# Block products in all four quarters of both MLPs, with sums that grow in PSUM, in a two-layer encoder on one core

## The chip, the core and the metric

The kernel runs on one core of a Trainium2 chip. TensorE (PE) multiplies, VectorE (DVE), ScalarE (ACT) and GpSimd (POOL) work element by element, and SyncE (SP) issues most of the transfers. Matmuls write to PSUM, which has eight banks of 128 x 512 fp32 values; everything else lies in SBUF. The metric is the device time of one execution in microseconds.

## What is computed

An encoder of two layers over a sequence of 512 with width 1024, all in fp32. Each layer is a mixer and an MLP, both behind an RMS norm and with a residual. The mixer of layer 0 is a stick-breaking attention, that of layer 1 a gated linear recurrence. The change touches both MLPs, the beginning of the recurrence and the final norm. Of the reference:

```python
def rms_norm(x, g):
    y = xf * lax.rsqrt(jnp.mean(xf * xf, axis=-1, keepdims=True) + EPS)
    return (y * g.astype(jnp.float32)).astype(x.dtype)
...
def rglru_block(h, w_in, conv_w, conv_b, w_a, b_a, w_x, b_x, lam, w_o):
    proj = h @ w_in
    gate = jax.nn.gelu(proj[..., :RG_WIDTH])
    xc = causal_depthwise_conv(proj[..., RG_WIDTH:], conv_w, conv_b)
...
def squared_relu_mlp(h, w1, w2):
    u = jax.nn.relu(h @ w1)
    return (u * u) @ w2
...
    for layer in range(DEPTH):
        h = rms_norm(x, norm_mix[layer])
...
        x = x + y
        h = rms_norm(x, norm_mlp[layer])
        x = x + squared_relu_mlp(h, mlp_w1[layer], mlp_w2[layer])
    return rms_norm(x, norm_final)
```

w1 is 1024 x 4096 and w2 is 4096 x 1024.

## The kernel before

**Numbers in two parts.** A matmul in full fp32 is replaced by three of a faster form: each operand is split into a high part (an ACT cast, `wh`, `xgh`, `bh`) and the remainder (a DVE subtraction, `wl`, `xgl`, `bl`), and high x high, low x high and high x low are added in PSUM (`three`, lines 193 to 197). A weight slab of 1024 x 128 (`slab`, line 174) is one transfer of 512 KB, a cast and a subtraction; `dense` (line 199) multiplies it with eight chunks of the input, 24 matmuls of 512 columns into one bank. `beside` (line 207) does so for several slabs at once, chunk by chunk, and takes the norm's matmul (line 149: ones times the sum of squares, then a square root on ACT and a reciprocal on DVE, line 126) in the middle.

**Order.** PE's instructions run in the order in which the program writes them. The orders of the other engines' queues are set by a scheduler that simulates the program and takes, among what is ready, what was written first; `issue_after` and `high_priority` bend that.

**The MLP.** The class `Mlp` (line 686) works in four quarters of the 4096 hidden features. For a quarter, `squared` makes its eight chunks `u`: 24 matmuls, then relu times the norm on DVE (line 739) and a square on ACT. The first three quarters are multiplied with w2 by Winograd's form of a 2 x 2 block product: seven products of halves in place of eight. `sums` (line 747) makes the sums of blocks of `u`, `split` their two parts; `load` (line 774) fetches the blocks b11, b12 and b22 of the weights, and `down` (line 791) goes through the seven products. For each it adds a second block to the first where that is wanted (line 805), splits it (`operand`, line 782) and issues 24 matmuls (lines 812 to 814) into two banks of its own, and then collects the two banks into the product's piece in SBUF: copies on ACT in the first quarter (line 818), additions on DVE later (line 820). The banks go round over all eight (`BANKS`, line 697). After the third quarter `outputs` (line 822) makes the four blocks of the output from the seven pieces, with seven DVE operations.

**The fourth quarter** is plain. `plain` splits the eight chunks of `u`. In layer 0 they are multiplied with slabs (`residual(w_m2, "mix1")`, line 878): 24 matmuls for each output chunk, and behind each of them the residual add (line 662), the scaling and split for the next layer (`halves`, lines 117 and 118) and the square. The block outputs are transposed on PE in the quarter's `squared` stage (`between`, lines 864 to 875) and added to `x` there. In layer 1 (lines 1085 to 1133) the rows of the result are made in two column halves of four row blocks each, 24 matmuls of 512 columns apiece, the last one as two of 256 columns; behind the second half stand the final norm and the stores.

**The recurrence's beginning.** `dense_in` (line 947) multiplies slabs of w_in. The first two go side by side with the norm's matmul in their middle (line 953). `conv` multiplies its bank with the norm (line 962) and reads it in four taps (lines 970 and 972), splits the result and loads and splits the gates' weights; `gates` multiplies with them. The order is that of the list in lines 1035 to 1041. From the seventh slab on, the low part is made on POOL with an adding transfer (lines 187 and 188).

## Time and profile before

| | us |
|---|---|
| median of 3 runs (lowest to highest) | 1085.01 (1083.53 to 1085.39) |
| profiled execution | 1085.11 |
| its span, first to last instruction | 1083.4 |

The profiled execution's time is 1.7 us over its span. Granted TensorE clock over the span: 0.999. In the page's rows of time, 40 slices of 27.1 us each, DVE is busy 0.7 or more in most slices, ACT in the first ones and around the recurrence. A row of the timeline gives start, length, engine, line, operation, output and inputs with shapes; an x says how many instructions were merged, and brackets tell how long the engine was idle before and what released it. A group's row gives busy us and mean ns. Matmul records overlap, so the distance between two starts is the pace, not the length.

### The profile page before, as it was taken

Reading aid. Unit: us, or ns where it says so; the run is one execution under the profiler, and the core shown is the slowest. Engines: PE = TensorE matmul, PEld = TensorE weight load, DVE = VectorE, ACT = ScalarE, POOL = GpSimd, SP = SyncE. Lnnn points to the kernel's source line nnn. Section 1 sums busy time; section 2 is a strip of 40 time slices with the busy share of each in tenths; the row PEclk is TensorE's granted clock in tenths of the full one; section 3 lists DMA queues with packets and bytes.
Section 4 is the critical chain, followed back from the end, with each engine's and each line's share of the span. In section 5 each row is a group of like instructions: output and inputs, shape, how many; then the busy total and the mean of one; then the engine's idle time right before and its main releaser. Section 6 shows DMA issues by size and latency. Waiting matters only on the chain.

```text
span 1083.4 us, 13612 instructions
## 1 busy us (share of the span) xinstructions
PE 1070.0 (99%) x5052; PEld 888.6 (82%) x5052; DVE 772.1 (71%) x1001; ACT 562.0 (52%) x831; POOL 202.5 (19%) x213
## 2 busy tenths in 40 slices
PE   8999999999999999999999999999999999999997
PEld 6888888788888888888888788888888888888886
DVE  7788787839894597599466658975784696699632
ACT  6767676726455344344345467944455443443422
POOL 2344443420000000002223556021000000002220
PEclk9999999999999999999999999999999999999999
DMA  7744453426205305302334486242215215203402
GB/s 230 189 128 137 124 149 96 156 82 246 84 26 187 98 20 175 117 1 80 114 111 136 90 209 153 82 175 78 78 59 175 78 47 184 81 1 123 150 1 78
DMA packets 43170, 122.57 MB, mean 113 GB/s; under 512 B 7648, under 2 KB 8416, under 8 KB 43104
## 3 DMA queue, kind: packets, MB, share of 16 engines
q1 hardware_dynamic: 41088, 115.94, 34.1%
q0 software_dynamic: 1440, 5.24, 2.6%
q8 instruction: 40, 0.66, 0.2%
q10 hardware_dynamic: 576, 0.52, 0.1%
q14 instruction: 26, 0.21, 0.1%
HBM read 101.76 MB, written 2.10 MB: 96 GB/s over the span
## 4 chain that ended last, share of the span: by engine, by line
PE 92%; DMA 2%; DVE 2%; ACT 2%; issue 1%; SPq 0%; DVEq 0%; ACTq 0%
PE ps_acc L195 7%; PE ps_acc L196 7%; PE ps_acc L197 7%; PE ps_o L195 4%; PE ps_o L196 4%; PE ps_o L197 4%; PE ps_t L196 4%; PE ps_t L195 4%; PE ps_t L197 4%; PE ps_z L195 3%; PE ps_z L196 3%; PE ps_z L197 3%; PE ps_t L813 2%; PE ps_t L812 2%; PE ps_t L814 2%; PE ps_acc L813 2%
## 5 line engine op out<-in xcount | busy, mean ns | idle before, releaser
L184 ACT CAST wh<-raw 128x1024 fp32r<-128x1024 f32 (+2 forms) x144 | 128.1, 911 | 158.9 <-PE ps_acc L197 51.2
L190 DVE TENSOR_TENSOR wl<-raw,wh 128x1024 fp32r<-128x1024 f32 (+2 forms) x134 | 141.4, 1070 | 27.4 <-ACT wh L184 27.4
L745 POOL TENSOR_TENSOR bl<-u,bh 128x512 fp32r<-128x512 f32 x16 | 30.5, 1904 | 584.9 <-ACT bh L744 569.8
L195 PE MATMUL ps_acc<-xgh,wh 128*128 128x512 f32 x320 | 129.1, 403 | 0.5 <-ACT wh L165 0.5
L787 ACT CAST wh<-b 128x1024 fp32r<-128x1024 f32 x72 | 75.5, 1049 | 98.4 <-PE ps_acc L814 15.7
L196 PE MATMUL ps_acc<-xgh,wl 128*128 128x512 f32 x320 | 125.4, 392 | 1.1 <-DVE wl L166 1.1
L197 PE MATMUL ps_acc<-xgl,wh 128*128 128x512 f32 x320 | 125.3, 392 | 0.1
L788 DVE TENSOR_TENSOR wl<-b,wh 128x1024 fp32r<-128x1024 f32 x72 | 87.9, 1221 | 25.3 <-ACT wh L787 25.2
L512 DVE TENSOR_TENSOR_SCAN scan<-keep,later 128x128 f32<-128x128 f32 (+1 forms) x64 | 58.4, 914 | 21.3 <-ACT keep L504 13.5
L197 PEld LDWEIGHTS ps_acc<-xgl,wh 128*128 128x128 f32 x320 | 60.1, 188 | 13.5 <-DVE xgl L118 0.5
L196 PEld LDWEIGHTS ps_acc<-xgh,wl 128*128 128x128 f32 x320 | 60.3, 188 | 12.0 <-DVE wl L166 1.8
L195 PEld LDWEIGHTS ps_acc<-xgh,wh 128*128 128x128 f32 x320 | 60.1, 188 | 11.7 <-ACT wh L165 0.7
L740 ACT ACTIVATE u<-u 128x512 f32<-128x512 f32 x64 | 39.3, 629 | 53.3 <-DVE u L739 53.1
L195 PE MATMUL ps_t<-xgh,wh 128*128 128x512 f32 x168 | 66.1, 394 | 0.0
L196 PE MATMUL ps_t<-xgh,wl 128*128 128x512 f32 x168 | 65.7, 391 | 0.0
L197 PE MATMUL ps_t<-xgl,wh 128*128 128x512 f32 x168 | 65.5, 390 | 0.0
L516 POOL TENSOR_TENSOR w<-w,scan 128x128 f32<-128x128 f32 (+1 forms) x64 | 53.8, 842 | 50.8 <-DVE scan L512 48.1
L195 PE MATMUL ps_o<-xgh,wh 128*128 128x512 f32 x152 | 60.2, 396 | 0.0
L197 PE MATMUL ps_o<-xgl,wh 128*128 128x512 f32 x152 | 59.2, 390 | 0.0
L196 PE MATMUL ps_o<-xgh,wl 128*128 128x512 f32 x152 | 59.2, 390 | 0.0
L195 PE MATMUL ps_z<-xgh,wh 128*128 128x512 f32 x128 | 50.0, 391 | 0.0
L196 PE MATMUL ps_z<-xgh,wl 128*128 128x512 f32 x128 | 49.9, 389 | 0.0
(356 smaller groups left out, 2768.1 us busy)
## 6 DMA issues: line engine op xcount, KB each, us to landing
raw<-in_w_m SPq DMA_DIRECT2D x72, 512.0 KB, 3.5
b<-in_w_dn SPq DMA_DIRECT2D x36, 512.0 KB, 4.3
raw<-in_w_in SPq DMA_DIRECT2D x16, 512.0 KB, 4.0
raw<-in_w_qk SPq DMA_DIRECT2D x12, 512.0 KB, 3.6
raw<-in_w_dn SPq DMA_DIRECT2D x12, 512.0 KB, 3.5
wl<-raw POOLq DMA_DIRECT2D x10, 512.0 KB, 6.3
x<-in_xT SPq DMA_DIRECT2D x16, 256.0 KB, 4.7
raw<-in_w_ro SPq DMA_DIRECT2D x8, 512.0 KB, 3.9
```

Of the source, the lines that this page charges most:

```text
L184: A.copy(wh[:, k, :], raw[:, k, :])
L190: V.tensor_tensor(wl[:, k, :], raw[:, k, :], f(wh[:, k, :]), ALU.subtract)
L195: PE.matmul(ps, wh, ah, start=start, stop=False)
L196: PE.matmul(ps, wl, ah, start=False, stop=False)
L197: PE.matmul(ps, wh, al, start=False, stop=stop)
L512: V.tensor_tensor_scan(sc[:, S - n : S][:, ::-1], keep[:, :n][:, ::-1], later[:, S - n :][:, ::-1], 1.0, ALU.mult, ALU.max,)
L516: G.tensor_tensor(wt, wt, sc[:, S - n + 1 : S + 1], ALU.mult)
L740: A.activation(t, t, AF.Square)
L745: G.tensor_tensor(bl[:, c, :], t, f(bh[:, c, :]), ALU.subtract)
L787: A.copy(wh, raw)
L788: V.tensor_tensor(wl, raw, f(wh), ALU.subtract)
L813: PE.matmul(ps[i], h[:, piece, ts], wl[:, jj, :], start=False, stop=False)
```

## The change

All four quarters of both MLPs use the block products, so w2 is stored in blocks as a whole and `w_m2` and `w_last` go.

The seven products are collected into four outputs, not seven pieces. Products that an output needs together grow in PSUM: P1, P6, P7 and P4 in one pair of banks (X), P5 and P3 in a second (V), P2 alone in a third (W). After each product the pair's sum so far is collected into one output, added or subtracted; an output's first collect in a layer is an ACT copy, all others are on DVE. `outputs` goes.

In the last quarter P1, P5 and P2 run first for one half of the inner index and then for the other, and P4 is left to a function of the layer (`end`). A block sum whose product is named in `far` is made by an adding transfer from HBM on POOL's queue (P7 and P4 in layer 0, P4 in layer 1).

Layer 0's `end` transposes output chunks 4 to 7 between the two halves of P4, with residual add and split; then the first two slabs of w_in run side by side over chunks 4 to 7 and 0 to 3, and chunks 0 to 3 are transposed after their first and second steps. The squares follow in a burst. The norm's matmul moves to the middle of the third slab, conv 3 ahead of the first gates, and the banks of `dense_in` go in the order t, t, acc, acc in place of alternating. The gates' weights are loaded three ahead.

Layer 1's `end` finishes the first two row blocks ahead of P4, and gives P4's last half two banks of 256 columns of its own, so that the sum in X is collected before them.

```diff
-    def beside(srcs, ah, al, pss, sq, at):
+    def beside(srcs, ah, al, pss, at, ks=range(C)):
         ws = [slab(src) for src in srcs]
-        for k in range(C):
-            if k == at:
-                r = sq.inv_rms()
+        for i, k in enumerate(ks):
+            if i in at:
+                at[i]()
             for ps, (wh, wl) in zip(pss, ws):
...
+        PRODUCTS = {
+            "P1": (0, "b11", None, "X", 0, False),
+            "P5": (4, "b11", "b12", "V", 3, False),
+            "P6": (5, "b11", "b22", "X", 1, True),
+            "P3": (6, "b22", None, "V", 1, False),
+            "P7": (1, "b12", "b22", "X", 3, True),
+            "P2": (2, "b21", None, "W", 0, False),
+            "P4": (3, "b11", "b21", "X", 2, False),
+        }
...
+        def block(self, q4, name, g, far):
+            _, b, to, *_ = self.PRODUCTS[name]
...
+            raw = self.raws[b, g]
+            if name in far:
+                G.dma_start(out=raw, in_=self.weights(q4, g, to), accum_op=ALU.add)
+            elif to:
+                V.tensor_tensor(raw, raw, self.raws[to, g], ALU.add)
+            return self.operand(raw)
+
+        def times(self, name, g, i, w, ps, new, cols=slice(0, S)):
+            block = self.PRODUCTS[name][0]
+            ts = slice(i * P, (i + 1) * P)
+            wh, wl = w
+            for jj in range(2):
+                h, l = self.a[2 * g + jj]
+                first, last = new and g == jj == 0, g == jj == 1
+                for n, (x, y) in enumerate(((h, wh), (h, wl), (l, wh))):
+                    PE.matmul(
+                        ps, x[:, block, ts], y[:, jj, cols], start=first and n == 0,
+                        stop=last and n == 2, skip_group_check=not new,
+                    )
+
+        def collect(self, name, i, ps, cols=slice(0, S)):
+            out, less = self.PRODUCTS[name][4:]
+            y = self.c[out][:, i, cols]
+            if (out, i) in self.begun:
+                V.tensor_tensor(y, y, ps, ALU.subtract if less else ALU.add)
+            else:
+                self.begun.add((out, i))
+                A.activation(y, ps, AF.Copy, scale=-1.0 if less else 1.0)
+
+        def down(self, q4, far=(), end=None):
+            sums = {}
+            def product(name, g):
+                w = self.block(q4, name, g, far)
+                to = self.PRODUCTS[name][3]
+                new = name in ("P1", "P5", "P2")
+                if to not in sums:
+                    sums[to] = [self.bank() for _ in range(2)]
+                for i in range(2):
+                    self.times(name, g, i, w, sums[to][i], new)
+                if g:
+                    for i in range(2):
+                        self.collect(name, i, sums[to][i])
+            if end is None:
+                for name in ("P1", "P5", "P6", "P3", "P7", "P2", "P4"):
+                    for g in range(2):
+                        product(name, g)
+                return
+            for g in range(2):
+                for name in ("P1", "P5", "P2"):
+                    product(name, g)
+            for name in ("P6", "P3", "P7"):
                 for g in range(2):
+                    product(name, g)
+            end([self.block(q4, "P4", g, far) for g in range(2)], sums["X"])
...
     with ExitStack() as mctx:
         mlp = Mlp(mctx, 0, sq)
+        def feature(c, tag):
+            pt = bank(tag)
+            for t in range(NB):
+                PE.transpose(
+                    pt[:, t * P : (t + 1) * P], mlp.y(t, c // 4)[:, c % 4 * P : (c % 4 + 1) * P],
+                    ident,
+                )
+            add_x(c, pt)
+            last["low"] = halves("mix1", c, x[c])
+
+        def end(ws, xs):
+            for i in range(2):
+                for g in range(2):
+                    mlp.times("P4", g, i, ws[g], xs[i], False)
+                mlp.collect("P4", i, xs[i])
+                if i == 0:
+                    for c in range(4, C):
+                        feature(c, "zzaa"[c - 4].replace("a", "acc"))
+
+        mlp.quarters(lambda q4, c: None, ("P7", "P4"), end)
+
+        begin = [bank("t") for _ in range(2)]
+        beside(
+            [w_in[C], w_in[C + 1]], xgh, xgl, begin,
+            {
+                1: lambda: [feature(c, "z") for c in range(2)],
+                2: lambda: [feature(c, "o") for c in range(2, 4)],
+            },
+            (*range(4, C), *range(4)),
+        )
+        sq = Squares()
+        with tc.tile_pool(name="squares", bufs=C - 1) as pool:
+            for c in range(C):
+                sq.chunk(c, x[c], last["low"], pool)
...
             if r is None:
-                first.extend(bank(t) for t in ("acc", "t"))
-                r = beside([w_in[C], w_in[C + 1]], xgh, xgl, first, sq, 4)
+                first.append(bank("acc"))
+                beside([w_in[C + 2]], xgh, xgl, first[2:], {4: norm})
             turns[0] += 1
             if first:
                 return first.pop(0)
-            return dense(w_in[i], xgh, xgl, tag=("t", "acc")[turns[0] % 2])
+            return dense(w_in[i], xgh, xgl, tag=("t", "t", "acc", "acc")[(turns[0] - 1) % 4])
...
-            (conv, 0), (conv, 1), (conv, 2), (gate, 0), (gates, 0), (gates, 1), (conv, 3), (gates, 2),
-            (gate, 1), (conv, 4), (gates, 3), (recur, range(3)), (gate, 2), (conv, 5), (gates, 4),
+            (conv, 0), (conv, 1), (conv, 2), (gate, 0), (conv, 3), (gates, 0), (gates, 1), (gate, 1),
+            (gates, 2), (conv, 4), (gates, 3), (recur, range(3)), (gate, 2), (conv, 5), (gates, 4),
...
+        def end(ws, xs):
+            for t in range(2):
+                square(t, 0, 0)
+                scaled(t, 0)
+                square(t, 1, 1)
+                finish(t, 1, 1)
+            for t in range(2, 4):
+                square(t, 1, 0)
+                scaled(t, 1)
+            for g in range(2):
+                mlp.times("P4", g, 0, ws[g], xs[0], False)
+            mlp.collect("P4", 0, xs[0])
+            square(2, 0, 1)
+            finish(2, 0, 1)
+            mlp.collect("P4", 1, xs[1])
+            for i in range(2):
+                cols = slice(i * HS, (i + 1) * HS)
+                ps = mlp.bank()[:, :HS]
+                for g in range(2):
+                    mlp.times("P4", g, 1, ws[g], ps, True, cols)
+                mlp.collect("P4", 1, ps, cols)
+                square(3, 0, 1 + i, cols)
+                if i == 0:
+                    V.tensor_tensor(ss[:, 3, 0:1], ss[:, 3, 0:1], ss[:, 3, 1:2], ALU.add)
+                    scaled(3, 0, cols)
+            finish(3, 0, 2, HS)
+
+        mlp.quarters(between, ("P4",), end)
```

`square` is the square with its row sum on ACT, `scaled` the product with the final norm's gain on POOL, and `finish` the rest of the final norm of a row block with its two stores; they hold the operations of lines 1110 to 1133.

More of the change, by code (lines that the diff above doesn't have):

```diff
@@ L757, in split @@
             if j < 2:
-                n = PIECES * HS
+                n = BLOCKS * HS
                 h, l = (
@@ L846, in quarters @@
                 if last:
+                    self.down(q4, far, end)
                     break
-                ts = [self.squared(q4 + 1, c) for c in range(2)]
+                for c in range(2):
+                    self.squared(q4 + 1, c)
                 self.down(q4)
-                if q4 + 1 == NQ - 1:
-                    self.blocks.close()
-                    self.outputs()
-                    for c in range(2):
-                        self.plain(c, ts[c])
-                else:
-                    self.sums(0)
-                    self.split(0)
+                self.sums(0)
@@ L860, in hybrid_encoder @@
+                self.split(0)
+            self.blocks.close()
     with ExitStack() as mctx:
         mlp = Mlp(mctx, 0, sq)
[L862 to L875 removed]
@@ L877, in hybrid_encoder @@
-        mlp.quarters(between)
-        sq = residual(w_m2, "mix1")
+        last = {}
+        def feature(c, tag):
[15 more added lines that the diff above has]
+                        feature(c, "zzaa"[c - 4].replace("a", "acc"))
@@ L1061, in hybrid_encoder @@
     with ExitStack() as mctx:
+        lp = mctx.enter_context(tc.tile_pool(name="last", bufs=1))
         mlp = Mlp(mctx, 1, sq)
```

202 lines of the change are left out of this document (63 added, 139 removed).

## The prediction, made before the change was run

> **What bounds the kernel now.** I read the page first, then who TensorE (PE) waited for, then the order of time around the stages that the diff touches.
>
> ```profile
> span 1083.4 us, 13612 instructions
> PE 1070.0 (99%) x5052; PEld 888.6 (82%) x5052; DVE 772.1 (71%) x1001; ACT 562.0 (52%) x831; POOL 202.5 (19%) x213
> PEclk9999999999999999999999999999999999999999
> ```
>
> ```profile
> PE ps_t L534 <- DVE tl L550: 2.5, 3, 1.5
> ...
> PE ps_z L495 <- ACT keep L504: 0.5, 1, 0.5
> ```
>
> PE has work in 99% of the span at full clock, and the list of its waits (us in total, times, longest) is short: the largest is 2.5 us, and every row belongs to the attention block or the start. From the first MLP on PE never waits. So the time is PE's instruction stream laid end to end, plus the start and the tail, and two questions decide: how much of that stream goes, and whether the rest still runs without gaps. Busy time can't answer the first, since records of neighbouring matmuls overlap; the distance from start to start can.
>
> ```profile
> 391.63 0.39 PE L812 MATMUL ps_o<-wh,bh 128*128 128x512 f32 x1
> 430.56 0.40 PE L195 MATMUL ps_z<-xgh,wh 128*128 128x512 f32 x1
> ...
> 548.46 1.03 PE L871 MATMUL ps_o<-ident,c 128*128 128x128 f32 x8
> 549.25 0.48 PE L195 MATMUL ps_acc<-bh,wh 128*128 128x512 f32 x1
> 592.89 0.39 PE L195 MATMUL ps_acc<-xgh,wh 128*128 128x512 f32 x1
> ...
> 1033.08 0.48 PE L1103 MATMUL ps_acc<-wh,bh 128*128 128x512 f32 x1
> 1071.27 0.28 PE L1103 MATMUL ps_t<-wh,bh 128*128 128x256 f32 x1
> 1076.90 0.28 PE L1105 MATMUL ps_t<-wh,bl 128*128 128x256 f32 x1
> ```
>
> **What is removed from PE.** These are PE's rows at the borders of stages. A block-product quarter (from line 812) has 7 products of 24 matmuls, 168 in all: 430.56 - 391.63 = 38.93 us, 0.2317 us each, 5.56 us a product. The plain fourth quarter of layer 0 has 8 x 24 = 192: 592.89 - 549.25 = 43.64 us, 0.2273 us each. In layer 1 it is 168 of 512 columns, 1071.27 - 1033.08 = 38.19 us, and 48 of 256 columns, 5.63 us from the first to the last and one step of 0.12 more: 43.94 us together.
>
> After the change layer 0 runs 168 in 38.93 us: 4.71 us less. In layer 1 the last 12 are cut into 24 of 256 columns: 156 x 0.2317 + 24 x 0.12 = 39.03 us, 4.91 us less. **PE's stream loses 9.6 us.** The transposes (32 a layer) move and stay as many; the pair of slabs run side by side, the third slab and the norm matmul that follow layer 0 stay as many too.
>
> The Trainium skill's "TensorE: Matmul & The Clock Gate" (section "Wait — 56ns, not 53.3ns?") gives a warm matmul its columns at 2.4 GHz and about 2.5 ns, 215.7 ns for 512 columns, whatever the pattern. By it the 48 fewer matmuls would be worth 10.4 us; the rows show 227 and 232 ns, with the block form the dearer, so I keep 9.6.
>
> **The sums that grow in PSUM.** Before, each product had two banks of its own out of eight, and was collected (line 820, VectorE, DVE; line 818, ScalarE, ACT, in the first quarter) while three more products ran. Now P1, P6, P7, P4 share one pair of banks and P5, P3 another. Each of P6, P3, P7 and P4 must wait in PE's queue until the collect of the product before in that pair has read it, and all later matmuls stand behind it. One other product lies between, 5.56 us of cover.
>
> ```profile
> 396.93 0.39 PE L814 MATMUL ps_o<-wh,sl 128*128 128x512 f32 x1
> 397.62 0.68 DVE L820 TENSOR_TENSOR c<-c,ps_o 128x512 f32<-128x512 f32 x1
> 398.55 0.68 DVE L820 TENSOR_TENSOR c<-c,ps_o 128x512 f32<-128x512 f32 x1
> ...
> 507.48 0.40 PE L812 MATMUL ps_t<-wh,bh 128*128 128x512 f32 x1
> 507.55 0.67 DVE L820 TENSOR_TENSOR c<-c,ps_o 128x512 f32<-128x512 f32 x1
> 509.29 0.67 DVE L820 TENSOR_TENSOR c<-c,ps_o 128x512 f32<-128x512 f32 x1
> ```
>
> ```profile
> 391.00:430.00 39.00, 39.00 (x170) 31.63 (x169) 30.82 (x36) 17.38 (x17) 0.00 (x0) 1.00 0.40 132
> 474.00:513.00 39.00, 39.00 (x170) 31.62 (x169) 36.29 (x38) 17.04 (x18) 4.43 (x2) 1.00 0.14 46
> 955.00:998.00 43.00, 43.00 (x187) 34.92 (x186) 40.26 (x42) 18.66 (x20) 5.64 (x2) 1.00 0.15 50
> ```
>
> The product whose last matmul starts at 396.93 is collected by 399.23, 2.1 us after its slot ends at 397.16; the latest I found ends at 509.96, 2.5 us after the next product began at 507.48. Both leave over 3 us. In the windows (length, then busy PE, weight loads, DVE, ACT, POOL) DVE has 30.8 of 39 us in the second quarter, and 36.3 and 40.3 in the third, where it also works off the seven output sums of line 829, which go away. The quarter that becomes a block quarter then has the load of the second. In the first quarter, DVE takes over 6 of 14 collects from ACT, 4 us of 39. I cost the seven quarters with the product between at nothing; the cover is those 3 us, and if it went, every us of lateness would be paid up to four times a quarter.
>
> The Trainium skill's "PSUM — Partial Sum Buffer" speaks against this edit: in "PSUM bank collisions raise a hardware error" two engines must not touch one bank in the same partitions at once, so that reading and resuming can't overlap. By that the wait is real and can't be softened; the rows say that it ends in time.
>
> In the last quarter of each layer P4 follows P7 at once, in the same banks. Cover is the second half of P7's last six matmuls, 1.39 us. The collect starts about 0.4 us after its bank's last matmul and takes 0.68, so a free DVE is in time by 0.3 us, and one in the middle of a 1.22 us subtraction is late by up to 0.9. I take 0.25 us a layer, **0.5 us** (0 to 1.8).
>
> The blocks fetched by an adding DMA on POOL's queue replace DVE additions.
>
> ```profile
> L787 ACT CAST wh<-b 128x1024 fp32r<-128x1024 f32 x72 | 75.5, 1049 | 98.4 <-PE ps_acc L814 15.7
> ...
> L788 DVE TENSOR_TENSOR wl<-b,wh 128x1024 fp32r<-128x1024 f32 x72 | 87.9, 1221 | 25.3 <-ACT wh L787 25.2
> ...
> wl<-raw POOLq DMA_DIRECT2D x10, 512.0 KB, 6.3
> ```
>
> Such a transfer lands in 6.3 us (median of ten). P4's can go when P6's operands are split, before P6 runs; P6, P3 and P7 are 16.7 us, and 6.3 us with a cast and a subtraction (1.05 and 1.22) leaves 8. Nothing is queued behind it on POOL there. Cost nothing.
>
> **Layer 0 to layer 1.** Before, each output chunk came with 5.4 us of matmuls to itself, and its residual add, scaling, split and square hid there. Now all eight come together: 4 chunks transposed between the halves of P4, 4 between the first matmuls of the next layer's two slabs. The nearest rows are those of the first MLP's start, which handles its chunks in such a burst.
>
> ```profile
> 244.30:267.30 23.00, 23.00 (x103) 18.90 (x102) 21.99 (x31) 17.25 (x25) 0.00 (x0) 1.00 0.69 252
> ...
> 255.93 0.68 DVE L662 TENSOR_TENSOR x<-x,ps_acc 128x512 f32<-128x512 f32 x1
> 256.53 2.73 DVE L118 SCALAR_TENSOR_TENSOR xgl<-x,colt,xgh 128x512 fp32r<-128x512 f32 x4
> 266.50 0.68 DVE L145 TENSOR_TENSOR ssq<-ssq,sq 128x512 f32<-128x512 f32 x1
> 267.44 1.02 PE L149 MATMUL ps_z<-ssq,ones 128*128 128x512 f32 x2
> ...
> L190 DVE TENSOR_TENSOR wl<-raw,wh 128x1024 fp32r<-128x1024 f32 x86 | 105.8, 1232 | 24.9 <-ACT wh L184 24.9
> ...
> L145 DVE TENSOR_TENSOR ssq<-ssq,sq 128x512 f32<-128x512 f32 x7 | 4.8, 688 | 0.1
> ```
>
> There DVE was busy 22.0 of 23 us, and the last square was added at 267.18, in time for the norm matmul by its usual 0.26 us. From the end of P4's first half PE now has 16 transposes (0.1 us each, from the eight at 548.46), 12 matmuls, 48 of the pair at 5.60 us per 24, 16 transposes and 12 of the third slab before the norm: 1.6 + 2.8 + 11.2 + 1.6 + 2.7 = 19.9 us. DVE has two collects, 8 adds, 8 splits, 7 sums of squares and three slabs: 1.4 + 5.4 + 5.5 + 4.8 + 3.7 = 20.8, and starts 0.5 us late: **1.4 us** of waiting. It shows at the second slab's bank, which P4's second collect frees, or at the norm. It is 0 if the slabs' subtractions wait their turn (17.6 us), and 4 if the collect of P4's second half stands behind the first chunks' eight operations, which come earlier in the program.
>
> The norm's result is late next.
>
> ```profile
> 598.49 1.02 PE L149 MATMUL ps_z<-ssq,ones 128*128 128x512 f32 x2
> 600.27 3.35 DVE L126 RECIPROCAL r<-r 128x512 f32<-128x512 f32 x1 [4.21 <-ACT r L125]
> 604.44 0.70 DVE L962 TENSOR_TENSOR ps_acc<-ps_acc,r 128x512 f32<-128x512 f32 x1 [0.82 <-PE ps_acc L197]
> 606.34 0.78 ACT L970 ACTIVATE bt<-ps_acc,colt 128x512 f32<-128x512 f32 x1
> 609.80 0.74 DVE L972 SCALAR_TENSOR_TENSOR bt<-ps_acc,colt,bt 128x509 f32<-128x509 f32 x1
> 612.21 2.14 DVE L979 TENSOR_TENSOR bl<-bt,bh 128x512 fp32r<-128x512 f32 x2 [0.41 <-ACT bh L978]
> ```
>
> It comes 603.62 - 598.49 = 5.1 us after the norm matmul starts, and the first convolution then takes 6.1 us (604.44 to 610.54) until its bank is free, 11.2 us in all. Before, PE had other banks. Now conv 3 takes conv 0's bank, and PE reaches it after 0.9 us of norm (its row, 1.02, overlaps the next), 2.7 us of the third slab and 5.46 of gate 0: 9.0 us. **2.2 us** of waiting; 0 if conv 0 runs alone (0.70 + 0.78 + 3 x 0.75 = 3.7 us after the result), 4.3 if a third chunk is interleaved (three operations of 0.7 more). The gates follow 5.4 us later, at 16.7, behind the two low halves (done 15.9 after the norm): nothing more.
>
> **The end.**
>
> ```profile
> 1077.22 0.42 DVE L1108 TENSOR_TENSOR c<-c,ps_t 128x256 f32<-128x256 f32 x1 [1.53 <-PE ps_t L1105]
> ...
> 1079.97 0.38 SPq L1133 DMA_DIRECT2D out<-c  x1
> ```
>
> The chain after the last matmul keeps its operations. But the row block before it is finished with 2.9 us of matmuls left in place of 5.7, on the same ACT, DVE and SP queue: **0.5 us**, between 0 and 2.
>
> **The sum.** The profiled execution took 1085.11 us, 0.1 over the median of 1085.01. 1085.11 - 9.6 + 0.5 + 1.4 + 2.2 + 0.5 = **1080.1 us**; its own range, with half of each bound, is 1077.5 to 1083.
>
> **Rivals.** First, every new wait is covered: 1085.1 - 9.6 = 1075.5. For it, the first MLP's start, where the same burst cost PE nothing; against it, the bank that conv 3 takes 2 us too early by the rows.
>
> Second, the passage between the layers costs its upper bounds: 4 + 4.3 + 1.8 + 2 = 12.1 against 9.6, so 1087.6, and 1085 with some of them. For it, DVE's 96% in the window above; against it, a late PE gives DVE time, so the first two don't add in full.
>
> Third, on the slow side, one mechanism: the collects come late and PE stands at each resumed sum. There are 4 in each of 8 quarters, 32; a mean wait of 0.3 us eats the gain, from 0.37 it is slower by more than 2.2 us, and 0.5 gives 1085.1 - 9.6 + 16 = 1091.5. For it, DVE's 40.3 of 43 us in layer 1; against it, the collects above, 3 us early. That the matmuls weren't the pace, so that their removal gives nothing, PE's list of waits excludes.
>
> **Chances.** Forecast 0.53, all covered 0.21, the passage dear 0.17, late collects 0.09. The range 1075 to 1086 takes in the second and most of the third, and leaves out the fourth. About 0.2%, 2.2 us, is what this measurement can tell from no change; faster takes the first two but for the forecast's upper edge at 1083: 0.71; within 0.12, from that edge and the dear passage at 1085; slower 0.17, the rest of the dear passage and the late collects.
>
> **What would show it.** Right: in each fourth quarter 168 matmuls and some 39 us; no PE waits at the resumed sums but P4's; a PE wait for DVE at the norm or the second slab's bank, and one of about 2 us at the first matmul of conv 3. Wrong: waits at P6, P3 or P7 in every quarter; a fourth quarter with waits for operands or for the adding DMAs; a tail over 8 us.

## The result, and the profile after

The changed kernel is slower by 0.4%: a median of 1088.66 us (1088.48 to 1089.49, 5 runs) beside 1084.77 for the kernel before, ratio 1.0041 with a 95% interval of 1.0026 to 1.0055. The forecast was 1080.1 us, with a range that ended at 1086. Its profiled execution took 1088.52 us. Page and list of PE's waits (us in total, times, longest) of the changed kernel:

```profile
span 1086.3 us, 13618 instructions
...
PE 1062.0 (98%) x4992; PEld 880.9 (81%) x4992; DVE 824.7 (76%) x1081; ACT 569.3 (52%) x823; POOL 167.1 (15%) x196
```

```profile
PE ps_t L193 <- DVE bt L1024: 5.9, 1, 5.9
...
PE ps_z L147 <- DVE ssq L143: 2.3, 1, 2.3
PE ps_t L824 <- DVE sl L776: 1.9, 1, 1.9
PE ps_t L193 <- DVE c L833: 1.2, 1, 1.2
...
PE ps_t L824 <- DVE c L833: 0.3, 1, 0.3
```

PE is busy for 8 us less than before, so the products did go; but a list that held nothing behind the attention block now holds four waits of over 1 us there, 11.3 us together. The row of a few tenths at line 824 is all that the resumed sums cost. Where the waits lie, PE's timeline shows, with the norm matmuls (line 147; 149 before) as marks:

```profile
265.73 0.59 PE L147 MATMUL ps_z<-ssq,ones 128*128 128x512 f32 x1
...
543.99 0.39 PE L824 MATMUL ps_t<-wh,bh 128*128 128x512 f32 x1
...
580.97 1.03 PE L897 MATMUL ps_z<-ident,c 128*128 128x128 f32 x8
...
587.55 0.50 PE L193 MATMUL ps_t<-xgh,wh 128*128 128x512 f32 x1 [1.19 <-DVE c L833]
...
604.90 1.29 PE L147 MATMUL ps_z<-ssq,ones 128*128 128x512 f32 x2 [2.30 <-DVE ssq L143]
...
621.90 0.77 PE L193 MATMUL ps_t<-xgh,wh 128*128 128x512 f32 x1 [5.94 <-DVE bt L1024]
...
751.53 0.59 PE L147 MATMUL ps_z<-ssq,ones 128*128 128x512 f32 x1
...
1050.34 0.50 PE L824 MATMUL ps_t<-wh,sl 128*128 128x512 f32 x1 [1.85 <-DVE sl L776]
...
1079.29 0.28 PE L824 MATMUL ps_o<-wh,sl 128*128 128x256 f32 x1
```

and of the kernel before, for the third mark:

```profile
743.12 0.59 PE L149 MATMUL ps_z<-ssq,ones 128*128 128x512 f32 x1
```

| from one start to the next, us | before | after | difference |
|---|---|---|---|
| begin to the norm of layer 0's MLP (same code) | 267.44 | 265.73 | -1.71 |
| on to the norm of layer 1's MLP | 475.68 | 485.80 | +10.12 |
| on to the last matmul | 333.78 | 327.76 | -6.02 |
| on to the end of the span | 6.49 | 6.97 | +0.48 |

The second stage holds layer 0's MLP, the passage and the recurrence. It should have lost 4.7 us and is 10.1 longer: 14.8 us are lost there. Its three waits are 9.4 of them. The windows of the changed kernel show more (length; busy us and count of PE, weight loads, DVE, ACT, POOL; granted clock):

```profile
605.67:609.08 3.41, 3.41 (x9) 2.42 (x8) 1.69 (x6) 2.71 (x3) 3.41 (x5) 0.50 0.10 40
609.10:615.60 6.50, 6.50 (x30) 5.20 (x28) 5.81 (x11) 2.12 (x4) 3.91 (x3) 1.00 0.95 176
...
619.32:626.15 6.83, 4.25 (x10) 3.41 (x11) 5.56 (x13) 0.65 (x2) 3.60 (x3) 0.50 0.55 108
```

Behind the wait at the norm the granted clock is 0.50 for 3.41 us, and at the wait of 5.9 us for 6.83 us, from 619.32, while PE still stands; between the two it is full. PE works for 3.41 + 4.25 us of this at half speed, which loses half of it, 3.8 us. The last 1.6 are two waits of 0.3 and 0.5 in layer 0's last products and the slow first matmul behind each wait.

What DVE and ACT did meanwhile:

```profile
595.58 3.00 DVE L143 TENSOR_TENSOR ssq<-ssq,sq 128x512 f32<-128x512 f32 x4
598.50 1.22 DVE L188 TENSOR_TENSOR wl<-raw,wh 128x1024 fp32r<-128x1024 f32 x1
599.63 0.69 DVE L143 TENSOR_TENSOR ssq<-ssq,sq 128x512 f32<-128x512 f32 x1
600.24 2.36 DVE L188 TENSOR_TENSOR wl<-raw,wh 128x1024 fp32r<-128x1024 f32 x2
602.51 2.25 DVE L143 TENSOR_TENSOR ssq<-ssq,sq 128x512 f32<-128x512 f32 x2
```

```profile
606.34 1.28 ACT L951 ACT_TABLE_LOAD   x1 [2.48 <-DVE ab L950]
607.63 0.21 ACT L951 ACTIVATE pp<-ab 128x8 f32<-128x8 f32 x1
607.86 1.28 ACT L123 ACT_TABLE_LOAD   x1
609.16 0.69 ACT L123 ACTIVATE r<-ps_z,eps_t 128x512 f32<-128x512 f32 x1
```

```profile
609.88 3.35 DVE L124 RECIPROCAL r<-r 128x512 f32<-128x512 f32 x1 [0.53 <-ACT r L123]
...
613.34 0.70 DVE L1014 TENSOR_TENSOR ps_t<-ps_t,r 128x512 f32<-128x512 f32 x1
...
614.54 0.69 DVE L1014 TENSOR_TENSOR ps_t<-ps_t,r 128x512 f32<-128x512 f32 x1
...
618.73 0.73 DVE L959 TENSOR_SCALAR pl<-pl 128x8 f32<-128x8 f32 x1
...
621.02 0.73 DVE L1024 SCALAR_TENSOR_TENSOR bt<-ps_t,colt,bt 128x509 f32<-128x509 f32 x1
```

Ahead of the norm stand three slab subtractions that PE needs only later (from 598.50), between the seven additions of squares. Behind it, ACT loads a table for a sigmoid of 128 x 8, then loads the square root's back, and only then works on the norm. The sigmoid belongs to the small operations that prepare the decay from lambda (lines 949 to 964, the same as before the change), and the others stand among the conv's taps. DVE has multiplied three chunks with the norm (613.34 to 615.23) before the first of their taps, so the taps of three chunks are interleaved. The kernel before had the sigmoid 45 us ahead of the norm, and the square root's table ready:

```profile
553.53 1.28 ACT L902 ACT_TABLE_LOAD   x1 [2.63 <-DVE ab L901]
...
595.30 1.28 ACT L125 ACT_TABLE_LOAD   x1
599.55 0.69 ACT L125 ACTIVATE r<-ps_z,eps_t 128x512 f32<-128x512 f32 x1 [2.96 <-PE ps_z L149]
```

By the program, their tiles lie in a pool that opens where layer 0's MLP closes: before, this was in the plain quarter, and now it is in the passage. Why the scheduler issued them no earlier is not shown: in the program as built, they take over bytes of a tile of `u`, whose last reader in the last quarter ends at 553.56 at the latest. Run 1 below tests only what their place costs.

In layer 1 the stage is 6.0 us shorter, more than its 4.9 us of products less a new wait of 1.9. The rest is pace, from the first matmul of a block quarter there to the first behind it:

```profile
801.40 0.39 PE L824 MATMUL ps_t<-wh,bh 128*128 128x512 f32 x1
...
839.48 0.39 PE L193 MATMUL ps_o<-xgh,wh 128*128 128x512 f32 x1
```

38.08 us for 168 matmuls, 0.2267 each; before the change, and in layer 0 after it (346.34 - 307.41), it was 38.93 and 0.2317.

### The profile page after: what moved, and what is told of

Its sections match the earlier page's. It is cut to its first block, busy times and chain, and to the rows that moved or that the text cites. A ratio compares the mean times of both kernels' runs of the same rounds, so it can differ in the third digit from the quotient of the medians.

```text
span 1086.3 us, 13618 instructions
## 1 busy us (share of the span) xinstructions
PE 1062.0 (98%) x4992; PEld 880.9 (81%) x4992; DVE 824.7 (76%) x1081; ACT 569.3 (52%) x823; POOL 167.1 (15%) x196
## 4 chain that ended last, share of the span: by engine, by line
PE 86%; DVE 7%; ACT 3%; issue 2%; DMA 2%; SPq 0%; DVEq 0%; ACTq 0%
PE ps_t L824 10%; PE ps_acc L193 6%; PE ps_acc L195 6%; PE ps_acc L194 6%; PE ps_o L824 6%; PE ps_z L824 6%; PE ps_acc L824 5%; PE ps_o L193 4%; PE ps_o L195 4%; PE ps_o L194 4%; PE ps_t L193 4%; PE ps_t L194 4%; PE ps_t L195 4%; PE ps_z L193 3%; PE ps_z L194 3%; PE ps_z L195 3%
## 5 line engine op out<-in xcount | busy, mean ns | idle before, releaser
L182 ACT CAST wh<-raw 128x1024 fp32r<-128x1024 f32 (+2 forms) x136 | 119.6, 902 | 129.9 <-PE ps_o L195 33.5
L795 ACT CAST wh<-b 128x1024 fp32r<-128x1024 f32 x96 | 100.9, 1051 | 141.0 <-PE ps_t L824 28.9
L188 DVE TENSOR_TENSOR wl<-raw,wh 128x1024 fp32r<-128x1024 f32 (+2 forms) x126 | 131.9, 1062 | 26.7 <-ACT wh L182 26.7
L796 DVE TENSOR_TENSOR wl<-b,wh 128x1024 fp32r<-128x1024 f32 x96 | 117.4, 1223 | 32.2 <-ACT wh L795 32.0
L810 POOL DMA_DIRECT2D b<-in_w_dn x6 | 5.4, 903 | 630.3 <-DVE wl L796 312.4
L194 PEld LDWEIGHTS ps_acc<-xgh,wl 128*128 128x128 f32 x312 | 59.2, 190 | 11.2 <-DVE wl L164 0.9
L193 PE MATMUL ps_o<-xgh,wh 128*128 128x512 f32 x160 | 63.3, 395 | 0.2 <-DVE x L658 0.2
L195 PE MATMUL ps_o<-xgl,wh 128*128 128x512 f32 x160 | 62.4, 390 | 0.0
L194 PE MATMUL ps_o<-xgh,wl 128*128 128x512 f32 x160 | 62.3, 389 | 0.0
L812 DVE TENSOR_TENSOR b<-b,b 128x1024 f32<-128x1024 f32 x46 | 56.1, 1220 | 0.2
L759 DVE TENSOR_TENSOR u<-u 128x256 f32<-128x256 f32 x128 | 49.6, 421 | 2.4 <-ACT u L749 1.9
```

Of the source, the lines that this page charges most:

```text
L182: A.copy(wh[:, k, :], raw[:, k, :])
L188: V.tensor_tensor(wl[:, k, :], raw[:, k, :], f(wh[:, k, :]), ALU.subtract)
L193: PE.matmul(ps, wh, ah, start=start, stop=False)
L194: PE.matmul(ps, wl, ah, start=False, stop=False)
L195: PE.matmul(ps, wh, al, start=False, stop=stop)
L759: V.tensor_tensor(u[:, out, :], u[:, x, :], u[:, y, :], op)
```

## The experiments

All times are beside the kernel before on the same chip (1084.4 to 1085.2 us); runs 1 to 4, 5 to 8, 9 to 12 and 13 to 15 share a chip each. The two stages are those of the table above, from the starts of the norm matmuls. The beginning, the same code in all kernels, took 265.2 to 268.9 us in the profiled executions, so the stages, from one profiled execution each, tell more than differences of 1 or 2 us between the medians.

| kernel | median us | ratio, 95% interval | norm to norm | norm to last matmul |
|---|---|---|---|---|
| before | 1084.77 | | 475.68 | 333.78 |
| changed | 1088.66 | 1.0026 to 1.0055 | 485.80 | 327.76 |
| 1 lambda early | 1086.89 | 1.0012 to 1.0033 | 484.54 | 327.69 |
| 2 other banks, gate 1 first | 1084.19 | 0.9985 to 1.0003 | 478.71 | 329.37 |
| 3 added matmuls | 1089.44 | 1.0029 to 1.0055 | 484.15 | 329.31 |
| 4 mixed layers | 1078.78 | 0.9937 to 0.9964 | 475.66 | 329.28 |
| 5 squares shared | 1087.84 | 1.0014 to 1.0041 | 483.37 | 327.73 |
| 6 = 1 + 2 + 5, conv 4 first | 1081.56 | 0.9964 to 0.9984 | 476.46 | 329.36 |
| 7 = 6, x earlier | 1083.03 | 0.9969 to 0.9988 | 476.73 | 329.52 |
| 8 changed + 4160 bytes | 1088.98 | 1.0028 to 1.0052 | 484.33 | 327.73 |
| 9 before + 96 bytes | 1080.02 | 0.9948 to 0.9975 | 473.04 | 332.23 |
| 10 = 4, 96 bytes, P7 by transfer | 1074.44 | 0.9888 to 0.9915 | 473.08 | 325.81 |
| 11 = 1 + 2 + 5, both edits of 10 | 1078.64 | 0.9931 to 0.9956 | 476.85 | 325.80 |
| 12 = 11, order of the change | 1073.17 | 0.9878 to 0.9905 | 470.86 | 325.84 |
| 13 other banks alone | 1086.66 | 1.0011 to 1.0028 | 483.05 | 327.75 |
| 14 = 12, lambda late | 1078.15 | 0.9919 to 0.9947 | 477.09 | 325.79 |
| 15 = 12, squares on DVE | 1076.14 | 0.9905 to 0.9930 | 473.56 | 325.82 |

**1. Lambda early.** `decays` holds lines 949 to 964, its tiles lie in the constant pool, and it stands behind a square of layer 0's second quarter:

```diff
+    def early_decays(q4, c):
+        if q4 == 1 and c == 4:
+            with tc.issue_after(mlp.mark.ins):
+                decays()
...
```

> The changed kernel, with the 28 small operations on lambda (lines 949 to 964, a sigmoid with its two table loads among them) issued in layer 0's second quarter in place of beside the norm. Theory, the norm's result is late by these: the wait at the first matmul of conv 3 falls from 5.9 us to 2 or 3, the granted clock is at half for one stretch less or a shorter one, and the time from 1088.5 to 1083 to 1085. Rival, the order of the conv operations on DVE sets conv 0's bank free: the wait falls by less than 1.5 us, and the time stays at 1087 or more.

Between the two: the wait at conv 3 fell to 3.8 us, the half clock stayed, and the time is 1.8 us lower, with intervals that overlap. So 2.1 us of the wait come from these operations; the rest doesn't. In this run the norm's result is there 6.0 us behind its matmul (604.81 to 610.81), and from DVE's first multiplication with it to the last tap of conv 0 it is still 8.7 us (610.91 to 619.58): three chunks are interleaved here too.

**2. Other banks.**

```diff
-        begin = [bank("t") for _ in range(2)]
+        begin = [bank("o") for _ in range(2)]
...
-                2: lambda: [feature(c, "o") for c in range(2, 4)],
+                2: lambda: [feature(c, "t") for c in range(2, 4)],
...
-                pi = bank("oozz"[turns[1] % 4])
+                pi = bank("zzoo"[turns[1] % 4])
...
-            (conv, 0), (conv, 1), (conv, 2), (gate, 0), (conv, 3), (gates, 0), (gates, 1), (gate, 1),
+            (conv, 0), (conv, 1), (conv, 2), (gate, 0), (conv, 3), (gate, 1), (gates, 0), (gates, 1),
...
-            begun[c] = bank("oozz"[c]), wh, wl
+            begun[c] = bank("zzoo"[c]), wh, wl
```

> The changed kernel with other banks only: the first two slabs of w_in go to the pair o, chunks 2 and 3 are transposed into t, gates take z, z, o, o, and gate 1 goes ahead of gates 0. So conv 3 has a bank that has long been read, and the second slab doesn't wait for P4's second collect. Theory, the price lies in two banks: the waits of 1.2 and 5.9 us and the second stretch of half clock (some 2.7 us) go, norm wait 2.3 to 3.6, 1088.5 becomes 1079 to 1081. Rival, DVE is the pace of the whole passage: the wait turns up at the first matmul of a later gate or conv, 3 us or more, and the time is 1085 or more.

Between the two: the waits at the second slab and at conv 3 and the half clock behind conv 3 went, 7.1 us norm to norm, but the norm still waited 2.3 us with half clock behind it, gates 2 waited 1.7, and layer 1's wait now had half clock behind it.

**3. Added matmuls.**

```diff
+        def warm(n):
+            ps = bank("o")
+            for _ in range(n):
+                PE.matmul(ps, xgh[:, 0, :P], xgh[:, 0, :], start=True, stop=True)
         def norm():
...
+            warm(10)
...
+            if c == 3:
+                warm(30)
```

> The changed kernel with added matmuls whose result nobody reads: 10 of 512 columns (2.3 us) before the norm's matmul and 30 (6.8 us) before conv 3, where PE stood still for 2.3 and 5.9 us. Theory, the idle time halves PE's clock afterwards (3.4 and 6.8 us at 0.5, about 4.3 us lost, of which the first 1.6 are hidden in the wait at conv 3): the granted clock stays at 1.0 all through, and the time falls by 2 to 3 us to 1085.5 to 1086.5. Rival, the clock's fall costs nothing beyond the waits or has another cause: the clock falls in the same places, time 1088.5 or more.

```profile
606.00:610.00 4.00, 4.00 (x17) 2.78 (x16) 2.29 (x5) 2.23 (x3) 4.00 (x5) 1.00 0.39 147
615.00:626.00 11.00, 10.02 (x45) 7.92 (x44) 10.86 (x26) 4.28 (x7) 4.58 (x4) 1.00 0.64 167
```

The windows behind the norm and around conv 3 have full clock, so its fall follows from standing still. Norm to norm gained 1.65 us, not 2 to 3, and the median nothing: layer 1's wait had half clock behind it (1.5 us), as in run 2. More than half of the 3.8 us that the clock takes in the passage is hidden behind the wait for DVE that comes next.

**4. Mixed layers.** Layer 0, passage and recurrence as before, layer 1 as after; `Plain` is the class of before.

```diff
-        mlp = Mlp(mctx, 0, sq)
+        mlp = Plain(mctx, 0, sq)
...
+        mlp.quarters(between)
+        sq = residual(w_m2, "mix1")
```

> Layer 0's MLP, the passage and the recurrence as before the change, layer 1's MLP with all quarters as block products as after it. Theory, all of the loss lies in the passage between the layers: layer 1 alone gives 4.9 us of products less 1.9 us of a new wait and 0.5 of tail, 2.5 us, and 2.5 more if the quicker pace of layer 1's block products (0.2267 in place of 0.2317 us a matmul) comes with its new program: 1079.8, or 1082.3 without the pace. Rival, layer 1 gives nothing by itself, and the gain seen there was made up by an offset from before: 1084 to 1085.

As the theory had it, with the pace: 1078.8. The whole loss lies between the two norms.

**5. Squares shared.**

```diff
-            for c in range(C):
-                sq.chunk(c, x[c], last["low"], pool)
+            A.activation(part, x[4], AF.Square)
+            for c in range(5, C):
+                A.activation(t, x[c], AF.Square)
+                G.tensor_tensor(part, part, t, ALU.add)
+            for c in range(4):
+                sq.chunk(c, x[c], last["low"], pool)
+            V.tensor_tensor(sq.acc, sq.acc, part, ALU.add)
```

> The changed kernel with the squares of chunks 4 to 7, which come first, summed on POOL as they come, and only four additions left on DVE behind the last split. Theory, the norm is late because DVE has seven additions (0.69 us each) between four slabs' subtractions: its wait falls from 2.3 to 0.5 us or less and no half clock follows it; conv 3's wait stays near 6 us or grows, since DVE sets it; time 2 to 3 us down, 1085.5 to 1086.5. Rival, POOL's additions slow DVE (one addition beside POOL's work took 1.52 us): the norm's wait stays over 1.5 us and the time at 1088 or more.

The norm's wait fell to 0.6 us, and conv 3's grew to 6.5: the gain went to the next wait for DVE, and 0.8 us of time were left, less than expected and less than the intervals can tell from nothing.

**6. All three**, with conv 4 also ahead of gates 2.

> The changed kernel with the early operations on lambda, the other banks, the squares shared with POOL, and conv 4 ahead of gates 2. Theory, the waits of the passage and the half clock behind them are its whole loss: of the 7.3 us that the kernel with other banks still lost there, norm wait 2.3, half clock 1.9 and gates 1.8 go, 1084.2 - 6.0 = 1078.2 (1077 to 1080), faster than before the change. Rival, DVE's work in the passage is the pace whatever the order: waits of 3 us or more turn up elsewhere between the norm and gates 3, and the time stays at 1081 or more.

Half right: faster than before the change, but 1081.6, where the rival begins. A new wait of 2.2 us stood at gates 5, on conv 5's high half, and layer 1's had half clock.

**7. x earlier.**

```diff
-            if q4 < NQ - 1 or c < 4:
+            if q4 < NQ - 1 or c > 5:
...
-                t = c - 4
+                t = c - 2
```

> The kernel of the run before, and in layer 1's last quarter the eight transposes of x with their additions come two chunks earlier. Theory, the wait of 1.9 us at the last split (and the half clock that followed it in three runs, 1.5 us) comes from these additions standing ahead of the split on DVE: the wait falls below 0.5 us, and the time by 1.5 to 3.4 against the run before, to 1075 to 1076.5. Rival, DVE is full there in any order: the wait stays over 1 us, and the two times differ by less than 1 us.

The rival holds for the wait: 2.1 us there, beside 1.9 in run 6. The transposes' additions are not the cause. The median is 1.5 us above run 6's, with intervals that overlap.

**8. 4160 bytes.**

```diff
+        spare = mctx.enter_context(tc.tile_pool(name="spare", bufs=1))
+        spare.tile([P, D + 16], F32, tag="spare", name="spare")
         mlp = Mlp(mctx, 0, sq)
```

> The changed kernel with 4160 unused bytes per partition set aside below layer 0's MLP, as the pool that layer 1 opens first does there; nothing else. Theory, where the operands lie in SBUF sets the pace of the block products: layer 0's go from 0.2317 to 0.2267 us a matmul, 0.85 us for each of four quarters of 168, and the time falls by 3.4 to 1085.2. Rival, the pace has another cause (the layer's data, or what runs beside): 0.2317 stays, and the time at 1088.5.

```profile
307.74 0.39 PE L824 MATMUL ps_t<-wh,bh 128*128 128x512 f32 x1
...
346.38 0.39 PE L193 MATMUL ps_o<-xgh,wh 128*128 128x512 f32 x1
```

38.64 us for layer 0's second quarter, 0.2300 a matmul: a pace of its own, neither 0.2317 nor 0.2267, and no gain in the median. So neither expectation came. The addresses explain why the pad missed: in the programs as built, the parts of u's last two pairs of chunks (`sh`, `sl`) lie 160 bytes modulo 256 from those of the weights before the change, 0 in layer 1 of the changed kernel, and 224 with this pad.

**9. 96 bytes** below each MLP of the kernel before, which makes it 0.

> The kernel before the change with 96 unused bytes per partition set aside below each MLP, nothing else. Theory, the distance in SBUF between the parts of u and those of the weights sets the pace of the block products: 160 bytes modulo 256 gave 0.2317 us a matmul, 224 gave 0.2300 in the run with 4160 bytes, 0 gave 0.2267 in layer 1 of the changed kernel. With 96 bytes it is 0 here: six quarters of 168 at 0.2267, 6 x 0.85 = 5.1 us less, 1079.5. Rival, the pace came with the changed kernel's program of layer 1: 0.2317 stays, and 1084.7.

```profile
389.76 0.39 PE L812 MATMUL ps_o<-wh,bh 128*128 128x512 f32 x1
...
427.84 0.39 PE L195 MATMUL ps_z<-xgh,wh 128*128 128x512 f32 x1
...
1026.73 0.48 PE L1107 MATMUL ps_acc<-wh,bh 128*128 128x512 f32 x1
...
1066.03 0.28 PE L1107 MATMUL ps_t<-wh,bh 128*128 128x256 f32 x1
```

All six block quarters take 38.08 us, and the kernel before gains 4.8 us by 96 bytes. The plain last quarter, all of whose operands the pad moved from a distance of 0 to one of 160 modulo 256, went the other way: 39.30 us for 168 matmuls where it had 38.19.

**10. Mixed layers, 96 bytes below layer 0's MLP,** and in layer 1 the second addition of P7 by transfer.

```diff
-        mlp.quarters(between, ("P4",), end)
+        mlp.quarters(between, ("P7", "P4"), end)
```

> The kernel with layer 0 as before the change and layer 1 as after it, with the 96 bytes below layer 0's MLP, and with P7's second block in layer 1's last quarter added by the transfer (as layer 0 has it) in place of two DVE additions of 1.2 us that stand ahead of the last split. Theory, the wait of 1.9 us there comes from DVE's load ahead of the split, and goes below 0.7 with these two; with it the half clock behind it (1.5 us); the 96 bytes give 3 x 0.85 = 2.5. 1078.8 becomes 1073 to 1075.5. Rival, the split comes late for another reason: the wait stays over 1.2 us, and 1076 to 1077 is left.

1074.4; the wait at the last split is gone from the list, and no half clock follows. P7's two additions of 1.2 us, ahead of that split on DVE, were its cause; the pad below layer 0 came with the same run, but the pad of run 8 left this wait at 1.9 us.

**11 and 12. All three edits, with both of run 10,** in two orders. Run 12 keeps the order of the change.

> The changed kernel with early operations on lambda, other banks, squares shared with POOL, gate 1 ahead of gates 0, gates 2 ahead of conv 4, the 96 bytes below layer 0's MLP and P7's second block added by the transfer. Theory, the wait of 2.2 us at gates 5 in the run of all three came from conv 4 ahead of gates 2 and goes; gates 2 waits 1.7 as in the run with other banks; the rest of the passage's waits is some 2 us. From the norm of layer 0's MLP to that of layer 1's 471 to 473 us (475.7 before the change), time 1073 to 1076, level with the kernel of mixed layers or below it. Rival, the passage always finds another DVE wait of 2 us or more: over 474 us there, and the mixed kernel stays ahead.

> The kernel of the run before, with gates 0 and 1 directly behind conv 3 as in the change, and gate 1 behind them. Theory, the first low half of the conv chunks is ready 15 to 16 us after the norm's matmul and PE arrives after 14.6: a wait of about 1 to 1.5 us at gates 0 and none at gates 2, so within 1 us of the run before. Rival, DVE lags further: 3 us or more at gates 0, and over 2 us slower than the run before.

Run 11 waits 4.4 us at gates 2, for ACT to read gates 0's bank, and takes 476.85 us between the norms: its rival. Run 12 was expected level with it or slower, and is 5.5 us faster, which neither theory nor rival had. Run 12's list of waits and its window over the norm and the conv chunks:

```profile
PE ps_t L530 <- DVE tl L546: 3.1, 4, 1.5
...
PE ps_z L147 <- DVE ssq L970: 0.6, 1, 0.6
PE ps_t L824 <- DVE c L833: 0.4, 1, 0.4
```

```profile
598.00:632.00 34.00, 33.20 (x140) 25.79 (x139) 23.99 (x35) 20.11 (x31) 22.00 (x15) 1.00 0.76 177
```

The largest wait is the attention's again; in the passage 0.6 us is the longest, at full clock. 1073.17 us is the fastest of all, though its interval overlaps with run 10's. On the same chip it is 6.9 us below the kernel before with its 96 bytes: that is what the change gives once its waits are gone, though 1.1 of it are what those bytes cost the plain last quarter (run 9).

**13, 14 and 15. One edit alone, or one out of the fastest.** Run 13 is the changed kernel with run 2's banks and its own order; 14 and 15 take lambda or the squares back out of run 12.

> The changed kernel with the other banks and nothing else: the order of conv, gate and gates is that of the change. Theory, the bank that conv 3 shares with conv 0 turns the late result of the norm into standing time, and gate 1 ahead of gates 0 was what held up gates 2 in the first run with other banks: nothing waits over 1.5 us between the norm and gates 3, and from the norm of layer 0's MLP to that of layer 1's it takes 476 to 478 us (485.8 in the changed kernel, 478.7 in the first run with other banks); time 1081 to 1084. Rival, the lambda operations hold up any order: gates 0 waits 3 us or more, over 479 us there, 1085 or more.

> The fastest kernel so far (1073.2) with the lambda operations back beside the norm, so everything but them. Theory, they delay the norm's result by the 2.1 us by which conv 3's wait shrank without them, and this shows at gates 0, the first to need a conv chunk: a wait of 1 to 2.5 us there, perhaps with half clock, 1074.5 to 1077. Rival, with a free bank for conv 3 they are covered: no wait over 0.5 us, 1073.

> The fastest kernel so far (1073.2) with all seven additions of squares back on DVE, so everything but the share of POOL. Theory, the norm waits 2.3 us again, 1.7 more than with POOL, and half clock may follow (up to 1.9): 1075 to 1077. Rival, what the norm loses is got back at the gates, which have other work ahead of them: within 0.5 us of 1073.

```profile
PE ps_z L1044 <- ACT bh L1030: 2.7, 1, 2.7
...
PE ps_o L1044 <- ACT bh L1030: 1.2, 1, 1.2
...
PE ps_z L1046 <- DVE bl L1031: 1.0, 1, 1.0
```

In run 13, above, the wait only moves from conv 3 to gates 0 and 1, 4.9 us in three pieces, half clock between them: the rival, though no single wait reaches its 3 us. In run 14, with 1.6, 1.1 and 1.0 us there,

```profile
614.70:626.00 11.30, 7.65 (x21) 4.95 (x20) 8.47 (x20) 6.20 (x10) 2.49 (x3) 0.70 0.71 157
```

the clock over that stretch is 0.70 and the kernel 5.0 us slower than run 12, more than expected. In run 15 the norm waits 2.4 us, the clock behind it stays full, and the time is 3.0 us up. Run 12 ran on another chip; each beside the kernel before on its own chip, the differences are 4.6 and 2.6 us.

## Why the prediction was wrong

**The products: right.** Layer 0's 156 matmuls up to the transposes took 36.98 us with 0.8 of waits, against 36.15 by the forecast's 0.2317. In layer 1 the 9.6 us were too few: a pace of 0.2267 gave 0.85 us more for each quarter, for a reason that has nothing to do with products (runs 8 and 9). What the forecast read as the price of the block form was the place of its operands.

**The resumed sums: right.** No wait at P6, P3 or P7, and 0.3 us at P4. The adding transfers cost nothing, as forecast; where the change kept DVE additions instead, in layer 1's P7, it paid 1.9 us at a split that the forecast did not look at (run 10).

**The passage, 1.4 us: too small.** The forecast named the second slab's bank and the norm as places for one wait; both came, 1.2 and 2.3 us, the first because P4's second collect stood behind the first chunks' eight operations, which the forecast had as its dear case. Its sum for DVE had three slabs, and three more subtractions stood among the additions of squares.

**The norm's result, 5.1 us behind its matmul: this step failed, and with it the 2.2 us at conv 3.** It took the chain of the kernel before as it stood: 5.1 us to the result and 6.1 for the first of two interleaved chunks. In the changed kernel the result came 8.3 us behind (604.90 to 613.23) and conv 0's bank was free at 16.9, not 11.2; PE, slowed by the half clock, came at 11.1, not 9.0, and waited 5.9 us, not 2.2. Two things made the chain longer. The change moved an unchanged piece of code into it: two table loads and some twenty small operations. And three chunks were interleaved, not two: 8.4 us for conv 0 (613.34 to 621.75), and 8.7 in run 1 without the lambda operations. The forecast had that case as its bound of 4.3 us for this wait; 3.8 were left in run 1. Taking the lambda operations out is worth 1.8 us alone, with intervals that overlap, and 4.6 where the other two edits are in. The bank named in the forecast was only where the delay showed: given another bank, PE waited at the gates (run 13).

**The clock: not in the forecast at all.** It priced a wait by its length. At the two waits of 2.3 and 5.9 us the half clock took 3.8 us more, of which full clock gave back 1.65 in run 3. The Trainium skill's "TensorE: Matmul & The Clock Gate" (section "What's actually happening") gives half clock after an idle window of some 3.4 us, in windows that run free; the two stretches of 3.41 and 6.83 us agree with one and two such windows. Its section "Why this matters for your kernels" warns of gaps above about 3 us; here a gap of 2.3 us was enough.

**The tail: right,** 0.5 us.

The rival of the dear passage was the nearest, in place and in time, 1087.6 us beside 1088.66. The time is in part luck: of its 12.1 us, 8.3 were for the passage, where 14.8 were lost between the norms, and layer 1's better pace and 1.7 us at the beginning, in the same code, made up for it. Its bounds left out the clock and the lambda operations. (Half-way from the forecast's terms to their bounds is 1077.8 to 1083.9, not the 1077.5 to 1083 that it gives; nothing hangs on that.)

One point stays open: with all waits gone the second stage of run 12 is 2.2 us shorter than that of run 9, where the products are worth 5.6 at equal pace (43.64 - 38.08), and PE's list has some 1.8 of the 3.4 between them; the rest was not followed up.

## What to carry to other kernels

When a stage that gave other work its cover goes, list everything the scheduler had put there, also code that the diff doesn't touch: table loads and small operations land on the next chain, here the norm's. On a kernel where PE never waits, price a wait of about 2 us or more with the half clock that may follow, and take waits out together, since one alone mostly moves to the next place. Before crediting an edit with a better pace, see whether it moved addresses.

## What the hardware showed that was not expected

A wait of the same length halved the clock in one run and not in another: layer 1's split was waited for 1.87 us in run 4 and 1.85 us in the changed kernel, and the windows behind it read

```profile
1039.60:1043.00 3.40, 3.40 (x8) 2.66 (x9) 1.82 (x3) 0.15 (x1) 0.90 (x1) 0.52 0.17 17
```

in run 4, and in the changed kernel

```profile
1050.40:1053.80 3.40, 3.40 (x15) 2.83 (x16) 2.76 (x4) 1.06 (x1) 0.90 (x1) 1.00 0.20 19
```

8 matmuls against 15 in the same time, 1.5 us. The traces' record of the granted clock shows why. In the changed kernel the clock is full for 600.75 us, half for 3.41, full for 10.24, half for 6.83 and full for 457.39: 176, 1, 3, 2 and 134 times 3.413 us. In all 17 traces the stretches between two changes are such multiples, so the changes fall on a grid of windows that runs free of the program. In run 4 the wait (1037.72 to 1039.59) lies whole in one window of the grid; in the changed kernel a border at 1049.40 cuts it (1048.48 to 1050.34) in two. The windows up to the border, run 4 first:

```profile
1036.34:1039.75 3.41, 1.54 (x8) 0.97 (x7) 3.41 (x4) 1.28 (x2) 0.00 (x0) 1.00 0.00 0
```

```profile
1045.98:1049.39 3.41, 2.50 (x12) 1.73 (x10) 3.41 (x4) 2.40 (x2) 0.00 (x0) 1.00 0.00 0
```

PE stood still for 1.87 us of the first and 0.91 of the second. Over the 17 traces, without their first 40 us and their ends, a window of full clock in which PE stood still for 1.85 us or more was followed by half clock, and one with up to 1.77 us was not; the one exception is a window with 1.89 us in run 6 (from 657.01). So the norm's wait of 2.3 us, whole in one window in the changed kernel, cost it half clock, and the same wait in runs 13 and 15, cut by a border, cost none.

The pace of fp32r matmuls of 512 columns, as the mean of a quarter, followed the distance of their operands in SBUF modulo 256 bytes, read from the programs as built: 0.2267 us at 0, and 0.2300 at 224 and 0.2317 at 160, where half of a quarter's matmuls lie so and the other half at 0. With all at 160, in run 9's plain quarter, it was 0.234 (39.30 us for 168). The halves show it within one product of the kernel before: its second half, with `sh` and `sl` at 160, takes 2.80 us for 12 matmuls (394.36 to 397.16), 0.2333 each. The first half, at 0, takes 0.2302 on the mean of the quarter's seven products and not 0.2267, so the distance of a matmul's own operands is not all of it. Three distances are no law, the pads also move what ACT and DVE write, and which port or bank stands behind it was not tried; but 96 unused bytes were worth 4.8 us to a kernel of 1085.
